# Keys by token: tensor-engine transposes in place of vector-engine block transposes

## The chip, the cores and the metric

The kernel runs on one core of a Trainium2 chip. The metric is the device time of one execution in microseconds, lower is better. The core has a tensor engine (TensorE, "PE" in the profile, with its weight loads as "PEld"), a vector engine (VectorE, "DVE"), a scalar engine (ScalarE, "ACT"), GpSimd ("POOL") and SyncE ("SP"), which issues the transfers. Each engine takes its instructions in order from its own queue and waits for the others by semaphores.

## What is computed

One layer of a hybrid decoder trunk on 2048 tokens of width 1024 in float32: RMS norm, one input projection to 3072 columns, two mixers side by side, an output projection with a residual add, a gated per-layer embedding and a final norm. The mixer that the change touches is a gated linear recurrence with four heads of 128 channels, cut to its core:

```python
b = jnp.cumsum(logf, axis=3)                 # log decays within a chunk
qe, ke = q * jnp.exp(b), k * jnp.exp(-b)
scores = where(causal, einsum('bhnck,bhnsk->bhncs', qe, ke), 0.0)
o_intra = einsum('bhncs,bhnsv->bhncv', scores, v)
dS = einsum('bhnsk,bhnsv->bhnkv', k * jnp.exp(b_last - b), v)
S[n + 1] = decay[n] * S[n] + dS[n]           # state of a head, 128 x 128
o = o_intra + einsum('bhnck,nbhkv->bhncv', qe, S)
```

The keys are needed in two layouts: with channels on the partitions for the scores, and with tokens on the partitions for the state update `dS`, because a matrix product sums over the partitions of both operands.

## The kernel before

The input projection and both mixers run first, for 1024 tokens at a time (`half(0)` and `half(1)`); a second phase does the output projection, the embedding and the last norm for 16 tiles of 128 tokens. Projections take float32 values in two parts of 12 significant bits, so that each product is three TensorE passes (`mm3`, lines 85 to 87).

In each half a list of units is worked through: `v` (values), `g` (output gates), `a` (the other mixer, four channel blocks), `fq` (decays, keys and queries of one head). A unit `fq` loads its weights and calls `unit_b(w, j, b)` for the two blocks of 512 tokens (`b` is 0 and 1), so there are 2 x 4 x 2 = 16 calls. One call does this:

- the projection `f` on TensorE; two sigmoids on ScalarE (`f` and `kn`, lines 431 and 432);
- a long run of VectorE work: the decay `f` (line 433), running products `cp` (438), their reciprocal `rc` (440), and at the end the scaled keys `kn` (455), 128 channels x 512 tokens;
- `transpose_blocks` (lines 199 to 204, used with `u2T` in the second phase too): 16 VectorE instructions, each of which transposes four 32x32 blocks, make `kT` from `kn` (lines 456 and 457);
- the projection `q` and its scaling;
- `scores` (line 469): four products of `kn` and `q` into the PSUM tile `sc`, masked into `sc_buf` by VectorE;
- `states` (line 477): four products of `kT` and the values into `ds` (line 480), then a chain over four chunks between ScalarE (`sp`, line 488) and VectorE (`state`, 489);
- `outputs` (line 493): products of `sc_buf` with the values and of `q` with the states (lines 496 and 499), and a norm;
- `finish` (line 513): four TensorE transposes `oT` (line 519), read by VectorE (`yb`, 521), and a transfer to DRAM.

The short pieces run some groups of products later: `after(n, fn)` notes a function, `tick()` at the end of each group runs what is due. That is the order in which the program is written. The order in which each engine's queue is filled is laid by a planner when the kernel is built: it simulates the engines with its own costs and takes, among what is ready by them, the piece that was written first. A product whose input is not ready by the planner's reckoning is so put behind others that are; on the chip the order is fixed.

PSUM has eight banks: three for projections (`pj`), three for `sc`, `ds`, `o` and the gates of unit `a` (`gl`), two in `tp`, which hold `oT` and the broadcast scales `rs` of the norm. A tile of a pool waits until the reader of the tile that had the buffer before it is done.

Of the kernel before, what the change touches and what calls it, by code (L numbers as in the profile page):

```python
# [8 lines left out]
F32 = mybir.dt.float32  # L9
# [7 lines left out]
# column blocks of the input projection, in the order in which the host lays them out  # L17
UNITS = [("v", 0), ("v", 1), ("fq", 0), ("g", 0), ("a", 0), ("fq", 1), ("a", 1), ("fq", 2), ("a", 2), ("g", 1), ("a", 3),
         ("fq", 3)]
P = 128  # L20
T = 2048
D = 1024
KT = D // P
NB = 512
# [3 lines left out]
# power of two that keeps the (masked) scores of later keys with earlier queries in range  # L28
DOWN = 2.0 ** -64
# columns of the packed per-channel vectors  # L30
# [5 lines left out]
def hymba_block(ctx: ExitStack, tc: tile.TileContext, x, xT, pT, w_in, vecs, rg_w, w_out, w_gate,  # L36
# [35 lines left out]
    def split(hi, lo, src, lo_eng):  # L72
        """src = hi + lo exactly, each with 12 significant bits."""
        nc.scalar.activation(hi, src, AF.Identity)  # L74
        lo_eng.tensor_tensor(lo, src, hi.bitcast(F32), ALU.subtract)  # L75

    def load_split(hi, lo, src, lo_eng, pool, tag, bufs, name):
        """hi + lo = src of DRAM, by way of a buffer of the given pool and tag."""
        raw = pool.tile(list(hi.shape), F32, tag=tag, name=f"raw_{name}", bufs=bufs)
        nc.sync.dma_start(raw, src)  # L80
        split(hi, lo, raw, lo_eng)

    def mm3(acc, lh, ll, rh, rl, first, last):
        """acc += (lh + ll)^T (rh + rl), without the product of the two low parts (under 2^-24)."""
        nc.tensor.matmul(acc, lhsT=lh, rhs=rh, start=first, stop=False)  # L85
        nc.tensor.matmul(acc, lhsT=lh, rhs=rl, start=False, stop=False)  # L86
        nc.tensor.matmul(acc, lhsT=ll, rhs=rh, start=False, stop=last)  # L87

# [13 lines left out]
    # the tensor engine reaches its full clock only after a while of work: products of constants until data is there  # L102
# [22 lines left out]
    def small_vectors():  # L125
        nc.sync.dma_start(vec, vecs[:, 0:NV])
        # softplus(-lambda) = max(-lambda, 0) + 2 atanh(y / (2 + y)), y = exp(-|lambda|)
        lam = vec[:, V_LAM:V_LAM + NH]
        c = [c1.tile([P, NH], F32, name=f"c{i}") for i in range(5)]
        nc.vector.tensor_scalar(c[0], lam, -1.0, 0.0, ALU.mult, ALU.max)  # L130
        nc.vector.tensor_scalar(c[1], lam, 0.0, None, ALU.min)
        nc.vector.tensor_tensor(c[1], c[1], c[0], ALU.subtract)
        nc.vector.scalar_tensor_tensor(c[1], lam, 0.0, c[0], ALU.max, ALU.add)
        nc.scalar.activation(c[2], c[1], AF.Exp, scale=-1.0)
        nc.vector.tensor_scalar(c[3], c[2], 2.0, None, ALU.add)
        nc.vector.reciprocal(c[3], c[3])
        nc.vector.tensor_tensor(c[2], c[2], c[3], ALU.mult)
        nc.vector.tensor_tensor(c[3], c[2], c[2], ALU.mult)
        nc.vector.tensor_scalar(c[4], c[3], 1.0 / 17, 1.0 / 15, ALU.mult, ALU.add)
        for n in (13, 11, 9, 7, 5, 3, 1):  # L140
            nc.vector.tensor_tensor(c[4], c[4], c[3], ALU.mult)
            nc.vector.tensor_scalar(c[4], c[4], 1.0 / n, None, ALU.add)
        nc.vector.tensor_tensor(c[4], c[4], c[2], ALU.mult)
        nc.vector.scalar_tensor_tensor(c[4], c[4], 2.0, c[0], ALU.mult, ALU.add)
        nc.vector.tensor_scalar(sp8, c[4], 8.0, None, ALU.mult)
        nc.vector.tensor_scalar(nsp8, c[4], -8.0, None, ALU.mult)
        # first row of softmax(hg_lb)
        l0, l1 = vec[:, V_LB0:V_LB0 + NH], vec[:, V_LB1:V_LB1 + NH]
        nc.vector.tensor_tensor(c[0], l0, l1, ALU.max)
        nc.vector.tensor_tensor(c[1], l0, c[0], ALU.subtract)  # L150
        nc.vector.tensor_tensor(c[2], l1, c[0], ALU.subtract)
        nc.scalar.activation(c[1], c[1], AF.Exp)
        nc.scalar.activation(c[2], c[2], AF.Exp)
        nc.vector.tensor_tensor(c[2], c[1], c[2], ALU.add)
        nc.vector.reciprocal(c[2], c[2])
        nc.vector.tensor_tensor(lb, c[1], c[2], ALU.mult)
        nc.vector.tensor_scalar(omlb, lb, -1.0, 1.0, ALU.mult, ALU.add)

    # Gate weights of the 8 blocks of 64 channels, in two parts: both gates side by side in the columns, and the
    # same rows twice, for the two parts of the block's channels.  # L160
# [9 lines left out]
    def inv_rms(pool, ss, tag):  # L170
        """1 / sqrt(mean + eps) of each partition, from the columns of ss that add up to its sum of squares."""
        ms = pool.tile([P, 1], F32, tag="ms", name=f"ms_{tag}", bufs=2)
        if ss.shape[1] > 1:
            nc.vector.tensor_reduce(ms, ss, AX.X, ALU.add)
            ss = ms
        nc.vector.tensor_scalar(ms, ss, 1.0 / D, EPS, ALU.mult, ALU.add)  # L176
        rs = pool.tile([P, 1], F32, tag="rs", name=f"rs_{tag}", bufs=2)
        nc.gpsimd.tensor_tensor(rs, ms, neg_half[:, 0:1], ALU.pow)  # L178
        return rs

    def rms_scale(pool, src, tag, junk):
        """1 / sqrt(mean(src^2) + eps) of each partition's row."""
        ss = pool.tile([P, 1], F32, tag="ss", name=f"ss_{tag}", bufs=2)
        nc.scalar.activation(junk, src, AF.Square, accum_out=ss)
        return inv_rms(pool, ss, tag)

    def resident(src, n, pool, kt, name, raw_pool, raw_tags):
        """Column half n of src in two parts, as [128, 512] tiles by row block. They may arrive in places of later
        tiles."""
        his, los = [], []  # L190
        for k in range(kt):
            his.append(pool.tile([P, NB], F32R, tag=f"hi{k}_{n}", name=f"{name}_hi{k}_{n}"))
            los.append(pool.tile([P, NB], F32R, tag=f"lo{k}_{n}", name=f"{name}_lo{k}_{n}"))
            rp, tag, bufs = raw_tags[k] if isinstance(raw_tags[k], tuple) else (raw_pool, raw_tags[k], 1)
            load_split(his[k], los[k], src[k * P:(k + 1) * P, n * NB:(n + 1) * NB],
                       nc.vector if k % 2 else nc.gpsimd, rp, tag, bufs, f"{name}{k}_{n}")
        return his, los

    def transpose_blocks(dst, src):
        """dst[:, k] = src[:, k]^T, 128 x 128, by 32 x 32 blocks on the vector engine."""  # L200
# [11 lines left out]
    # Short pieces of tensor engine work whose inputs take a while run some groups of products later.  # L212
# [3 lines left out]
    def after(n, fn):  # L216
        later.append((clock[0] + n, fn))
# [27 lines left out]
    def prep_u(hf, tt, rs=None):  # L245
        """u = rms_norm(x) of 128 tokens, channel-major, in two parts."""
# [20 lines left out]
    def load_w(hf, n, between=None, raw_pool=None, *raw_tags):  # L267
        """A block of 256 columns of the input projection, in two parts."""
# [12 lines left out]
    def begin():  # L281
        """The first values need no scaled input: of two tiles, x times the norm's weight, in two parts, and the
        scales, by which the products are multiplied."""
# [26 lines left out]
    def half(hf):  # L310
# [15 lines left out]
        def v_tiles(w, pair, t2):  # L326
            """Values of two heads for 256 tokens, token-major."""
# [31 lines left out]
        def unit_a(w, j):  # L359
# [20 lines left out]
            def recur():  # L380
                # a = exp(-8 r sp); 1 - a^2 = tanh(8 r sp) (1 + a^2)
# [19 lines left out]
            for b in range(2):  # L401
# [9 lines left out]
                # the two parts of each 64 channels, one above the other  # L411
# [11 lines left out]
        def unit_b(w, j, b):  # L423
            """Gated linear recurrence of head j on one block of 512 tokens, in chunks of 128 whose decays are
            taken relative to the middle of the chunk."""
# [8 lines left out]
            # running products of the decays from the start of each 64  # L434
# [19 lines left out]
            # keys  # L454
            nc.vector.scalar_tensor_tensor(kn, kn, omlb[:, j:j + 1], rc, ALU.mult, ALU.mult)
            kT = bp.tile([P, NB], F32, tag="kT", name=f"kT_{nm}", bufs=2)
            transpose_blocks(kT.rearrange("p (n s) -> p n s", n=4), kn.rearrange("p (n s) -> p n s", n=4))
            tick()
            # queries
# [9 lines left out]
            def scores():  # L469
# [5 lines left out]
                after(1, lambda: states(sc))  # L475

            def states(sc):
# [15 lines left out]
            def outputs(sc, sps):  # L493
# [6 lines left out]
                # norm over the head's values, per token  # L500
# [59 lines left out]
    def load_y(tt, pool, bufs, raw_pool, raw_tag):  # L560
        """One tile of mixer outputs in two parts, and of the residual stream."""
# [57 lines left out]
    def gate(tt, uh, ul, h):  # L619
# [10 lines left out]
        # the last tile ends on narrower pieces, whose chain is shorter  # L630
# [24 lines left out]
    def split_u2(tt, last):  # L655
        """u2T of a tile in two parts; those of the last tiles take the place of mixer outputs."""
# [33 lines left out]
def _layout(inp):  # L690
# [5 lines left out]
    # by 64 channels: the two gates' weights side by side, in the other order for every second block  # L696
# [37 lines left out]
```

## Time and profile before

| | us |
|---|---|
| median of 3 runs | 1103.26 |
| lowest and highest of them | 1098.7 to 1104.31 |
| profiled execution: span from first to last instruction | 1104.0 |
| its TensorE busy | 1044.5 |
| its VectorE busy | 814.9 |
| its ScalarE busy | 451.1 |
| its GpSimd busy | 278.3 |

The profiled execution is an execution of its own; its time is told by its span, which holds the whole of it. Busy time is the time in which an engine has an instruction under way. Matrix products overlap in the pipeline, so a busy TensorE is not TensorE at its peak. An idle engine costs time only where the work that sets the end waits for it.

### The profile page before, as it was taken

The page shows a single profiled execution, that of the slowest core. Times are in us where ns is not written, and L with a number is a line of the kernel's source. Part 1 is how long each engine was busy: PE and PEld are TensorE (multiplying, and loading weights), DVE is VectorE, ACT ScalarE, POOL GpSimd, SP SyncE. Part 2 cuts the span into 40 slices and gives each one's busy share as a digit, 9 for nine tenths or more (in the row PEclk, how much of TensorE's full clock was granted, in tenths as well). Part 3 has the DMA queues.
Part 4 walks back from the last instruction along what each step waited for, and adds up shares of the span by engine and source line. Part 5 has one row for each costly group of instructions (what it writes and reads, how often), then busy time and mean ns, then how long its engine had stood idle before and what let it go on. Part 6 is the DMA issues. An engine that isn't in the chain of part 4 may idle for free.

```text
span 1104.0 us, 13904 instructions
## 1 busy us (share of the span) xinstructions
PE 1044.5 (95%) x5128; PEld 874.3 (79%) x5128; DVE 814.9 (74%) x1629; ACT 451.1 (41%) x763; POOL 278.3 (25%) x238
## 2 busy tenths in 40 slices
PE   8899899898898999999989899899999999999997
PEld 7888788687777998788778788667888888888886
DVE  5846946979799706965979969899766666666664
ACT  4546336455556325535545226642222222222222
POOL 4131221222222132221222216651112221111110
PEclk8999999999899999999999999899999999999999
DMA  8421111111135211111112128441122222211101
GB/s 324 135 77 39 58 58 39 57 58 58 57 115 204 102 58 58 58 58 39 58 48 67 33 82 273 128 158 63 64 84 77 72 67 67 67 63 57 43 29 49
DMA packets 55267, 91.10 MB, mean 83 GB/s; under 512 B 4640, under 2 KB 25120, under 8 KB 55200
## 3 DMA queue, kind: packets, MB, share of 16 engines
q1 hardware_dynamic: 55200, 90.22, 24.0%
q8 instruction: 40, 0.66, 0.2%
q14 instruction: 27, 0.22, 0.1%
HBM read 73.43 MB, written 16.78 MB: 82 GB/s over the span
## 4 chain that ended last, share of the span: by engine, by line
PE 54%; DVE 30%; DMA 4%; ACT 4%; issue 4%; POOL 2%; SPq 0%; POOLq 0%; DVEq 0%; ACTq 0%
DVE kT L203 7%; PE g L86 6%; PE g L87 6%; PE g L85 6%; PE o L87 4%; PE o L86 4%; PE o L85 4%; DVE rc L440 4%; PE v L87 2%; PE v L86 2%; DMA raw_w<-in_w_in 2%; PE v L85 2%; PE ga L87 2%; PE ga L85 2%; PE ga L86 2%
## 5 line engine op out<-in xcount | busy, mean ns | idle before, releaser
L75 POOL TENSOR_TENSOR wlo<-raw_w,whi 128x512 fp32r<-128x512 f32 x92 | 133.5, 1461 | 330.8 <-ACT whi L74 330.8
L203 DVE STREAM_TRANSPOSE u2T<-u 32x256 f32<-32x256 f32 x256 | 111.7, 436 | 3.8
L87 PE MATMUL o<-wo_hi,yl 128*128 128x512 f32 x256 | 102.4, 401 | 3.5 <-POOL yl L75 3.5
L85 PE MATMUL o<-wo_hi,yh 128*128 128x512 f32 x256 | 101.3, 396 | 0.7 <-ACT yh L74 0.7
L86 PE MATMUL o<-wo_lo,yh 128*128 128x512 f32 x256 | 101.6, 397 | 0.0
L86 PE MATMUL g<-wg_lo,u2uh 128*128 128x512 f32 x224 | 89.2, 398 | 2.6 <-DVE wg_lo L75 2.6
L85 PE MATMUL g<-wg_hi,u2uh 128*128 128x512 f32 x224 | 89.2, 398 | 1.4 <-ACT wg_hi L74 1.4
L87 PE MATMUL g<-wg_hi,u2ul 128*128 128x512 f32 x224 | 88.6, 396 | 0.0
L74 ACT ACTIVATE whi<-raw_w 128x512 fp32r<-128x512 f32 x96 | 57.7, 624 | 72.4 <-DMA raw_w<-in_w_in 63.6
L203 DVE STREAM_TRANSPOSE kT<-kn 32x128 f32<-32x128 f32 x256 | 77.4, 302 | 3.4
L488 ACT ACTIVATE sp<-state,dec 128x128 f32<-128x128 f32 x60 | 23.9, 400 | 115.5 <-DVE state L489 66.0
L87 PE MATMUL v<-whi,ul 128*128 128x256 f32 x224 | 63.8, 286 | 3.4 <-DVE ul L75 3.4
L75 POOL TENSOR_TENSOR yl<-raw_y,yh 128x512 fp32r<-128x512 f32 x32 | 45.4, 1422 | 84.1 <-ACT yh L74 84.1
L86 PE MATMUL v<-wlo,uh 128*128 128x256 f32 x224 | 63.5, 284 | 0.6 <-POOL wlo L75 0.6
L85 PE MATMUL v<-whi,uh 128*128 128x256 f32 x224 | 63.6, 285 | 0.0
L87 PEld LDWEIGHTS o<-wo_hi,yl 128*128 128x128 f32 x256 | 48.6, 190 | 15.1 <-POOL yl L75 4.0
L406 DVE TENSOR_SCALAR xc<-xa,vec 128x512 f32<-128x512 f32 x16 | 11.4, 711 | 64.7 <-ACT xa L404 64.5
L85 PEld LDWEIGHTS o<-wo_hi,yh 128*128 128x128 f32 x256 | 48.6, 190 | 12.6 <-ACT yh L74 1.2
L86 PEld LDWEIGHTS o<-wo_lo,yh 128*128 128x128 f32 x256 | 48.5, 189 | 12.2
L178 POOL TENSOR_TENSOR rs_f<-ms_f,neg_half 128x1 f32<-128x1 f32 x16 | 8.8, 551 | 190.2 <-DVE ms_f L176 177.2
L74 ACT ACTIVATE yh<-raw_y 128x512 fp32r<-128x512 f32 x32 | 19.9, 629 | 86.3 <-issue 53.9
L641 ACT ACTIVATE gt<-gt 128x512 f32<-128x512 f32 (+1 forms) x33 | 20.2, 611 | 83.0 <-DVE gt L640 83.0
(219 smaller groups left out, 2956.9 us busy)
## 6 DMA issues: line engine op xcount, KB each, us to landing
raw_w<-in_w_in SPq DMA_DIRECT2D x96, 256.0 KB, 2.9
xcm<-in_xT SPq DMA_DIRECT2D x18, 512.0 KB, 4.0
xt<-in_x SPq DMA_DIRECT2D x16, 512.0 KB, 5.4
raw_y<-y_dram SPq DMA_DIRECT2D x32, 256.0 KB, 2.8
h<-in_x SPq DMA_DIRECT2D x16, 512.0 KB, 3.4
out<-h SPq DMA_DIRECT2D x15, 512.0 KB, 2.6
y_dram<-ga SPq DMA_DIRECT2D x16, 256.0 KB, 2.4
y_dram<-yb SPq DMA_DIRECT2D x16, 256.0 KB, 2.1
```

Of the source, the lines that this page charges most:

```text
L74: nc.scalar.activation(hi, src, AF.Identity)
L75: lo_eng.tensor_tensor(lo, src, hi.bitcast(F32), ALU.subtract)
L85: nc.tensor.matmul(acc, lhsT=lh, rhs=rh, start=first, stop=False)
L86: nc.tensor.matmul(acc, lhsT=lh, rhs=rl, start=False, stop=False)
L87: nc.tensor.matmul(acc, lhsT=ll, rhs=rh, start=False, stop=last)
L178: nc.gpsimd.tensor_tensor(rs, ms, neg_half[:, 0:1], ALU.pow)
L203: nc.vector.transpose(dst[32 * j:32 * j + 32, :, 32 * i:32 * i + 32], src[32 * i:32 * i + 32, :, 32 * j:32 * j + 32])
L406: nc.vector.tensor_scalar(xc[:, s], xa[:, b * NB:b * NB + NB], cw[:, 0:1], vec[:, V_CONVB + j:V_CONVB + j + 1], ALU.mult, ALU.add)
L440: nc.vector.reciprocal(rc, cp)
L488: nc.scalar.activation(sp, state[j], AF.Identity, scale=dec[:, n])
L641: nc.scalar.activation(gt, gt, AF.Sigmoid)
```

## The change

`transpose_blocks` is no longer called in `unit_b`. In `scores`, behind the mask, four TensorE transposes of 128x128 take `kn` to a PSUM tile `pk` of the pool `tp`, and one ScalarE copy takes `pk` to `kT` in SBUF. `states` gets `kT` as an argument. `transpose_blocks` stays for `u2T`. Comments are taken out elsewhere.

```diff
             nc.vector.scalar_tensor_tensor(kn, kn, omlb[:, j:j + 1], rc, ALU.mult, ALU.mult)
-            kT = bp.tile([P, NB], F32, tag="kT", name=f"kT_{nm}", bufs=2)
-            transpose_blocks(kT.rearrange("p (n s) -> p n s", n=4), kn.rearrange("p (n s) -> p n s", n=4))
             tick()
...
                 nc.vector.copy_predicated(sc, keep.bitcast(U32), psc.rearrange("p (n t) -> p n t", n=4))
-                after(1, lambda: states(sc))
-
-            def states(sc):
+
+                pk = tp(f"kT_{nm}")
+                for c in cs:
+                    nc.tensor.transpose(pk[:, c], kn[:, c], ident)
+                kT = bp.tile([P, NB], F32, tag="kT", name=f"kT_{nm}", bufs=2)
+                nc.scalar.activation(kT, pk, AF.Identity)
+                after(1, lambda: states(sc, kT))
+
+            def states(sc, kT):
                 pds = gl(f"ds_{nm}")
                 for n, c in enumerate(cs):
                     nc.tensor.matmul(pds[:, c], lhsT=kT[:, c], rhs=vt[:, 4 * b + n, hc], start=True, stop=True)
```

## Rows read from the trace of the kernel before

**Rows 1.** The page's busy time of each engine: us, share, instructions.

```profile
PE 1044.5 (95%) x5128; PEld 874.3 (79%) x5128; DVE 814.9 (74%) x1629; ACT 451.1 (41%) x763; POOL 278.3 (25%) x238
```

**Rows 2.** The page's chain that ended last, by engine and by line.

```profile
PE 54%; DVE 30%; DMA 4%; ACT 4%; issue 4%; POOL 2%; SPq 0%; POOLq 0%; DVEq 0%; ACTq 0%
DVE kT L203 7%; PE g L86 6%; PE g L87 6%; PE g L85 6%; PE o L87 4%; PE o L86 4%; PE o L85 4%; DVE rc L440 4%; PE v L87 2%; PE v L86 2%; DMA raw_w<-in_w_in 2%; PE v L85 2%; PE ga L87 2%; PE ga L85 2%; PE ga L86 2%
```

**Rows 3.** Windows: stretch, length, busy PE PEld DVE ACT POOL, clock, DMA, GB/s.

```profile
60.00:360.00 300.00, 279.22 (x1381) 234.39 (x1380) 233.60 (x476) 152.43 (x234) 78.19 (x62) 0.98 0.22 76
360.00:660.00 300.00, 285.65 (x1531) 245.57 (x1530) 218.25 (x453) 126.10 (x198) 69.57 (x51) 0.98 0.17 57
```

**Rows 4.** Waits of TensorE: us in total, times, longest.

```profile
PE ds L480 <- DVE kT L203: 22.3, 13, 3.6
PE sc L472 <- DVE kn L455: 10.2, 6, 2.0
```

**Rows 5.** Timeline of TensorE: start, us, instruction, idle before and its releaser.

```profile
196.96 1.13 PE L480 MATMUL ds<-v,kT 128*128 128x128 f32 x8 [0.57 <-DVE kT L203]
...
214.19 1.13 PE L472 MATMUL sc<-q,kn 128*128 128x128 f32 x8 [1.56 <-DVE kn L455]
...
220.31 1.16 PE L480 MATMUL ds<-v,kT 128*128 128x128 f32 x8 [2.97 <-DVE kT L203]
...
614.64 2.08 PE L480 MATMUL ds<-v,kT 128*128 128x128 f32 x8 [3.07 <-DVE kT L203]
```

**Rows 6.** Timeline of VectorE between 190 and 222 us.

```profile
191.77 5.04 DVE L203 STREAM_TRANSPOSE kT<-kn 32x128 f32<-32x128 f32 x16
196.84 0.67 DVE L433 TENSOR_SCALAR f<-f,omlb,lb 128x512 f32<-128x512 f32 x1
...
197.57 2.17 DVE L394 TENSOR_TENSOR i<-i,th 128x1024 f32<-128x1024 f32 x1
...
213.30 0.74 DVE L455 SCALAR_TENSOR_TENSOR kn<-kn,omlb,rc 128x512 f32<-128x512 f32 x1
...
215.22 5.04 DVE L203 STREAM_TRANSPOSE kT<-kn 32x128 f32<-32x128 f32 x16
```

**Rows 7.** Windows of the six half-clock stretches, first and sum, columns as above.

```profile
136.52:139.94 3.42, 3.42 (x14) 2.94 (x13) 1.99 (x6) 0.40 (x1) 1.02 (x1) 0.50 0.00 0
...
sum 23.91, PE 22.91 PEld 20.11 DVE 21.70 ACT 2.53 POOL 2.71; mean PE 3.82 PEld 3.35 DVE 3.62 ACT 0.42 POOL 0.45
```

**Rows 8.** Groups of instructions: busy us, mean ns, idle before and releasers.

```profile
L203 DVE STREAM_TRANSPOSE kT<-kn 32x128 f32<-32x128 f32 x256 | 77.4, 302 | 3.4
...
L519 PE MATMUL oT<-ident,on 128*128 128x128 f32 x60 | 9.1, 272 | 0.0
...
L404 ACT ACTIVATE xa<-xa 128x512 f32<-128x512 f32 x14 | 8.3, 591 | 9.5 <-PE xa L87 9.3
```

**Rows 9.** Timeline of ScalarE, around 194 and around 212 us.

```profile
194.30 1.06 ACT L391 ACTIVATE th<-th 128x1024 f32<-128x1024 f32 x1
...
209.69 0.40 ACT L488 ACTIVATE sp<-state,dec 128x128 f32<-128x128 f32 x1 [2.06 <-DVE state L489]
...
213.41 0.40 ACT L488 ACTIVATE sp<-state,dec 128x128 f32<-128x128 f32 x1 [1.30 <-DVE state L489]
214.73 1.28 ACT L415 ACTIVATE xp<-xc 64x512 fp32r<-64x512 f32 x2 [0.92 <-DVE xc L409]
```

**Rows 10.** Timeline of TensorE: two groups of `oT`, the next `sc`.

```profile
228.88 0.60 PE L519 MATMUL oT<-ident,on 128*128 128x128 f32 x4
229.32 0.39 PE L499 MATMUL o<-sp,q 128*128 128x128 f32 x2
...
238.73 0.60 PE L519 MATMUL oT<-ident,on 128*128 128x128 f32 x4
...
251.68 1.05 PE L472 MATMUL sc<-q,kn 128*128 128x128 f32 x8
```

**Rows 11.** Timeline of VectorE: the reader of the second.

```profile
244.69 0.75 DVE L521 SCALAR_TENSOR_TENSOR yb<-oT,vec,gb 128x512 f32<-128x512 f32 x1
```

## The prediction

> **What bounds the kernel now.** I read the page first. TensorE is busy 95% of the span and VectorE 74% [rows 1], so over the whole run TensorE is nearly full; but the chain that ended last spends 30% of its time on VectorE, and its largest single entry is `kT`, the sixteen block transposes of line 203 [rows 2]. Both can be true only if TensorE is the limit for most of the time and VectorE for short stretches, so the next view is busy time by stretch. From 60 to 660 us, where all 16 calls of `unit_b` lie, TensorE is idle 20.8 + 14.4 = 35.2 us [rows 3]. The view of waits names who ends that idleness: line 480 (`ds`, which reads `kT`) waits 22.3 us in 13 places, line 472 (`sc`, which reads `kn`) 10.2 us in 6 [rows 4]. 32.5 of the 35.2 us are thus VectorE's keys coming late. All else that holds TensorE there is 2.7 us.
>
> The timeline of TensorE shows the form of it [rows 5]. It comes in pairs, once for each head: on the first block of 512 tokens `ds` waits little (0.57 at 196.96). On the second block `sc` waits 1.56 at 214.19, short output products and two projection products follow, and then `ds` waits 2.97 at 220.31. The last of these second waits is 3.07 at 614.64. I read all 13: the seven of second blocks add up to 18.8, the six of first blocks to 3.5. The near constant 3 us has a plain reading in VectorE's own timeline [rows 6]: `kn` starts at 213.30 and is followed by one convolution step and one gate product, then come sixteen transposes from 215.22 that take 5.04 us, and `ds` starts in the very moment they end (220.3). TensorE ran out of work at 220.31 - 2.97 = 217.34, some 2 us after `sc` ended (214.19 + 1.13 = 215.32), so 3 us are left over. The order was laid down as if the transposes were cheaper than they are.
>
> The gaps cost a second time. Directly after six of these pairs, or between their two waits, the granted clock is 0.50 for a stretch [rows 7]: the stretches add up to 23.9 us with TensorE busy 22.9 us in them, at the level of 1.2 GHz in place of 2.4. At full clock that work takes half, so 22.9 / 2 = 11.5 us are lost. Idle and half clock together: 22.3 + 10.2 + 11.5 = 44.0 us is what late keys cost in this execution.
>
> **The change part by part.** I sum against the profiled execution, whose span is 1104.0; the median of the runs shown, 1103.26, lies 0.1% below, so I forecast on the same scale.
>
> *Removed: 256 block transposes.* 77.4 us of VectorE at 302 ns each, 16 x 0.302 = 4.8 in sum and 5.04 by the clock for a call [rows 6, 8]. They aren't worth 77 us, because TensorE works under most of them. They are worth the waits that end on them: the 22.3 us of `ds` go as far as they are a wait for line 203. Term: -22.3.
>
> *Moved earlier: what stood behind the transposes on VectorE.* Between 190 and 222 VectorE has hardly a free moment (the transposes at 191.77 are followed at 196.84 by the next block's `f`, and so on to `kn` at 213.30 [rows 6]). Without the 5 us at 191.77, the chain to the second block's `kn` can start up to 5 us earlier, but `i` (line 394) in that queue needs the square root that ScalarE ends at 194.30 + 1.06 = 195.36 [rows 9], against its start at 197.57 now, so in an unchanged order only about 2.2 us are won. The `sc` wait there is 1.56, so it could vanish. On the other side the planner lays the order again: it takes its own, too small, cost of the transposes out and may bring `sc` forward with `kn`, which keeps the wait. Bounds 0 and -10.2; nothing tells which is nearer, so I take the middle. Term: -5.
>
> *Added on TensorE: 64 transposes of 128x128 f32.* The kernel has the same instruction already, `oT` at line 519, four to a call: the mean is 272 ns [rows 8], but they overlap: four start at 228.88 and the next product starts at 229.32, 0.44 us later [rows 10]. 16 x 0.45 = 7.2. TensorE is the limit, so all of it counts. Term: +7.2. The upper bound is no overlap at all, 64 x 0.272 = 17.4.
>
> The Trainium skill speaks against this part: "TensorE: Matmul & The Clock Gate", section "PE-mode transpose", puts such a transpose at about 275 ns inside a kernel. The row's 272 ns agrees, but the starts in the trace lie 0.11 apart. By the page's figure as an estimate the term would be 64 x 0.275 = 17.6 in place of 7.2, and the result about 1091.
>
> *Added on ScalarE: 16 copies of 128x512 from PSUM.* Line 404 is that copy, 591 ns [rows 8]: 9.5 us in all, on an engine busy 152 and 126 of 300 us [rows 3]. Being busy little hides the work, not the delay: `ds` now waits for transposes, then copy, and ScalarE's queue is in order. Ahead of the copy in a first block stands that square root, which ends at 195.36; `ds` there is at 196.96 now [rows 5], so a copy behind it (195.4 to 196.0) is ready in time, and one behind another 0.6 us piece a few tenths late. In a second block there are the last `sp` of the block before (213.41) and the two `xp` at 214.73, which waited 0.92 for VectorE [rows 9]. With `sc` at about 213, transposes until 214.5 and a copy of 0.6, `kT` is there between 215.2 and 216.6, while TensorE has those 2 us of output products to run. Bounds for a call: 0 (hidden by those products) and 1.3 (the copy stands behind an `sp` that waited 1.30). The first is nearer, since both queues give room; I take 0.25 on the mean. Term: 16 x 0.25 = +4.
>
> *The two buffers of `tp`.* The new transposes share them with `oT`, whose reader is `yb` on VectorE. The `oT` at 238.73 is the last of its head and is read from 244.69 to 245.4; the next head's first `sc` stands at 251.68 [rows 10, 11]. So the buffers are free 6 us before they are wanted, and I take nothing; if that cover went, a late `yb` would stop TensorE itself for up to the 6 us between 238.73 and 244.69.
>
> *The clock.* With the 3 us hole gone and the `sc` hole halved, I expect about four of the six half-speed stretches to go. Bounds 0 and -11.5. Term: -7.
>
> Sum: 1104.0 - 22.3 - 5 + 7.2 + 4 - 7 = 1080.9, so **1081**. The boundary between the halves and everything from 660 us on have their own work; I let them move up unchanged.
>
> **The rivals.**
> *All of it comes back.* `sc` never waits, the copy is always hidden, the clock never falls: 1104.0 - 22.3 - 10.2 - 11.5 + 7.2 = 1067. For it: VectorE loses 77 of its 234 + 218 = 452 us between 60 and 660 us [rows 3]. Against: the holes exist because the order is planned on costs that differ from the chip's, and reciprocals and scans stay.
> *The hole stays half open.* `sc` waits as before and `ds` waits 1 us for the copy in each call: -22.3 + 16 + 7.2, with half the clock losses back (-5.7): 1099. For it: ScalarE waits 1.3 and 2.1 us in front of `sp` in just these stretches [rows 9].
> *Slower: the wait only changes hands.* The copy is planned behind an `sp` or `xp` that hangs on VectorE, so `ds` waits in total as long as now (22.3 us, 1.4 for each call), and TensorE has the transposes on top: 1104.0 + 7.2 = 1111. It decides from a mean wait of 1.3 us for each call: then -22.3 + 16 x 1.3 + 7.2 = +5.7, over half a per cent. Against: only the copies of second blocks meet such a queue.
> *Transposes do not overlap here.* If the four run one after the other as their 272 ns say, the term is 17.4, not 7.2: 1081 + 10.2 = 1091. Against it stands the pitch in [rows 10]. The Trainium skill's section named above gives the same result.
> That VectorE is not relieved at all can be left out: line 203 keeps only `u2T`.
>
> **How the numbers follow.** Half a per cent (5.5 us) is about what a measurement of this kernel tells from no change. Chances: the forecast (1072 to 1090) 0.58; all of it (1063 to 1072) 0.12; half open (1090 to 1104) 0.16, of which half lies below 1097.7; wait changes hands (1105 to 1115) 0.08; transposes in series 0.06. Faster by over 0.5%: 0.58 + 0.12 + 0.08 + 0.06 = 0.84. Slower by over 0.5%: three quarters of the changed hands, 0.06. Within: 0.10. The range 1066 to 1099 leaves out some of the best case, the upper part of the half-open one and the slower one, near 2 in 10; the likeliest alone is 1072 to 1090.
>
> **What would show it.** In the profile of the changed kernel: no `kT` at line 203, VectorE busy near 815 - 77 = 737; 64 single transposes into a `kT` tile on TensorE with starts 0.11 apart; 16 ScalarE copies near 0.6 us. Right, if line 480 waits under 6 us in all, names ScalarE as releaser, and the granted clock from 60 to 660 is 0.99 or more. The `sc` term is right if line 472 waits between 3 and 8 us. Wrong, if `ds` waits over 1 us for the copy in most calls, if a transpose waits for `yb`, or if a new wait appears in stretches that were full before, because the order was laid anew.

## The result and the profile after

The changed kernel takes 1090.0 us (median of 4 runs, 1087.67 to 1091.96) against 1102.41 us (4 runs, 1098.7 to 1104.31) for the kernel before on the same chip: a ratio of 0.9876, 95% interval 0.9852 to 0.9899. That is 13.7 us faster (0.0124 x 1104), inside the predicted range, where 23 us were forecast. The profiled execution has a span of 1088.5 us, 15.5 less than before.

The page's busy time and its chain, beside [rows 1, 2]:

```profile
PE 1043.3 (96%) x5192; PEld 878.2 (81%) x5192; DVE 739.3 (68%) x1373; ACT 459.4 (42%) x779; POOL 272.1 (25%) x238
...
PE 73%; DVE 15%; DMA 5%; ACT 3%; issue 2%; POOL 1%; SPq 1%; POOLq 0%; DVEq 0%; ACTq 0%
```

VectorE has lost 75.6 us and its share of the chain is halved. TensorE's part of the chain went from 54% to 73%. The windows of the two stretches, beside [rows 3], and the view of TensorE's waits from 60 to 660 us, beside [rows 4]:

```profile
60.00:360.00 300.00, 287.59 (x1481) 244.57 (x1480) 206.79 (x380) 161.12 (x248) 78.96 (x64) 0.99 0.25 83
360.00:660.00 300.00, 291.86 (x1564) 251.37 (x1563) 182.55 (x306) 133.99 (x216) 68.01 (x52) 0.99 0.19 61
```

```profile
PE sc L470 <- DVE kn L455: 16.7, 7, 3.1
PE o L503 <- ACT sp L492: 2.1, 3, 1.4
```

TensorE's idle time there fell from 35.2 to 12.4 + 8.1 = 20.5 us. The wait of `ds` for the transposed keys, 22.3 us before, is gone altogether. But the other wait on late keys, `sc` for `kn`, rose from 10.2 to 16.7 us, and it is nearly all that is left: seven waits, one at the second block of each of seven heads. TensorE's timeline around the pair of [rows 5] shows it:

```profile
190.49 1.05 PE L470 MATMUL sc<-q,kn 128*128 128x128 f32 x8
191.38 0.60 PE L476 MATMUL kT<-ident,kn 128*128 128x128 f32 x4
...
196.85 1.06 PE L484 MATMUL ds<-v,kT 128*128 128x128 f32 x8
...
206.87 1.13 PE L470 MATMUL sc<-q,kn 128*128 128x128 f32 x8 [2.39 <-DVE kn L455]
207.84 0.60 PE L476 MATMUL kT<-ident,kn 128*128 128x128 f32 x4
208.28 0.61 PE L500 MATMUL o<-v,sc_buf 128*128 128x128 f32 x4
...
212.62 1.06 PE L484 MATMUL ds<-v,kT 128*128 128x128 f32 x8
```

The four transposes stand directly behind `sc`, the next product starts 208.28 - 207.84 = 0.44 us after them, and neither `ds` shows a wait. The keys do come sooner, as VectorE's timeline shows, beside [rows 6]:

```profile
187.14 0.74 DVE L455 SCALAR_TENSOR_TENSOR kn<-kn,omlb,rc 128x512 f32<-128x512 f32 x1
...
191.57 1.22 DVE L438 TENSOR_TENSOR_SCAN cp<-f,d 128x512 f32<-128x512 f32 x1
193.53 0.06 DVE L393 MEMSET th<- 128x1 f32 x1 [0.73 <-ACT th L391]
193.62 1.22 DVE L394 TENSOR_TENSOR i<-i,th 128x1024 f32<-128x1024 f32 x1
...
205.99 0.74 DVE L455 SCALAR_TENSOR_TENSOR kn<-kn,omlb,rc 128x512 f32<-128x512 f32 x1
```

For comparison, the first block's `sc` in TensorE's timeline of the kernel before:

```profile
192.34 1.05 PE L472 MATMUL sc<-q,kn 128*128 128x128 f32 x8
```

Count from that `sc` in each kernel. The second block's `kn` started 213.30 - 192.34 = 21.0 us behind it before, and 205.99 - 190.49 = 15.5 us now: 5.5 us sooner, near the 5.04 us of one call's block transposes. TensorE, though, reaches the second block's `sc` (its start less its wait) 212.63 - 192.34 = 20.3 us behind it before, and 204.48 - 190.49 = 14.0 us now: 6.3 us sooner. The newly laid order has fewer projection products between the two: from the first block's `ds` to the second block's `sc` there were 64, and now there are 29. So TensorE asks earlier by more than the keys are earlier, and the wait grows from 1.56 to 2.39 us. The other six heads that wait show the same in the timelines: on the mean of the seven, the keys come 4.8 us sooner and TensorE asks 5.7 us sooner, and seven times the difference of 0.93 is the 6.5 us by which the wait grew.

The stretches of half clock between 60 and 660 us, the first of three and their sum, beside [rows 7]:

```profile
127.33:130.74 3.41, 3.41 (x19) 3.41 (x18) 1.02 (x3) 1.40 (x3) 0.00 (x0) 0.50 0.26 98
...
sum 10.23, PE 10.23 PEld 10.23 DVE 4.64 ACT 4.09 POOL 0.00; mean PE 3.41 PEld 3.41 DVE 1.55 ACT 1.36 POOL 0.00
```

Six stretches have become three, and the loss went from 11.5 to 10.2 / 2 = 5.1 us. The tile `kT` in the changed kernel (durations are minimum, median and maximum in ns, then first and last start in us):

```profile
L476 PE MATMUL kT<-ident,kn x64: 270/273/421, 111.1 to 617.7; 128*128 128x128 f32 x64
L478 ACT ACTIVATE kT<-kT x16: 577/584/607, 113.1 to 620.6; 128x512 f32<-128x512 f32 x16
```

The second phase only moved up. The product of line 85 that waits for `yh` stands in TensorE's timeline of the kernel before at

```profile
704.44 0.50 PE L85 MATMUL o<-wo_hi,yh 128*128 128x512 f32 x1 [0.73 <-ACT yh L74]
```

and in that of the changed kernel at

```profile
688.63 0.50 PE L85 MATMUL o<-wo_hi,yh 128*128 128x512 f32 x1 [0.45 <-ACT yh L74]
```

15.8 us earlier, which is the whole difference of the spans. The terms by the profile are -22.3 (`ds`), +6.5 (`sc`), +7.2 (transposes, taken at the prediction's 16 x 0.45) and -6.3 (clock), in sum -14.9. The small other waits rose from 2.7 to 20.5 - 16.7 = 3.8 us, which makes it -13.8: 2 us of the 15.8 aren't accounted for.

### The profile page after: what moved, and what is told of

It reads as the page before. It is cut to its first block, busy times and chain, and to the rows that moved or that the text cites. A ratio compares the mean times of both kernels' runs of the same rounds, so it can differ in the third digit from the quotient of the medians.

```text
span 1088.5 us, 13796 instructions
## 1 busy us (share of the span) xinstructions
PE 1043.3 (96%) x5192; PEld 878.2 (81%) x5192; DVE 739.3 (68%) x1373; ACT 459.4 (42%) x779; POOL 272.1 (25%) x238
## 4 chain that ended last, share of the span: by engine, by line
PE 73%; DVE 15%; DMA 5%; ACT 3%; issue 2%; POOL 1%; SPq 1%; POOLq 0%; DVEq 0%; ACTq 0%
PE g L86 7%; PE g L87 7%; PE g L85 6%; PE o L87 4%; PE o L86 4%; PE o L85 4%; DVE rc L440 3%; PE v L87 2%; PE v L86 2%; PE v L85 2%; PE q L86 2%; PE q L85 2%; PE q L87 2%; PE f L87 2%; PE f L86 2%
## 5 line engine op out<-in xcount | busy, mean ns | idle before, releaser
L75 POOL TENSOR_TENSOR wlo<-raw_w,whi 128x512 fp32r<-128x512 f32 x92 | 125.6, 1379 | 303.6 <-ACT whi L74 303.2
L440 DVE RECIPROCAL rc<-cp 128x512 f32<-128x512 f32 x16 | 53.6, 3348 | 0.2
L86 PEld LDWEIGHTS g<-wg_lo,u2uh 128*128 128x128 f32 x224 | 42.3, 189 | 13.2 <-DVE wg_lo L75 2.6
```

The source lines that it names most:

```text
L440: nc.vector.reciprocal(rc, cp)
```

## The experiments

Ratios are to the kernel before on the same chip, with 95% intervals; the changed kernel has 0.9876 [0.9852, 0.9899]. A difference of ratios is turned into time with 1104 us. Waits are those of TensorE from 60 to 660 us. Two questions come out of the profile: whether the wait of `sc` can be had back by asking later, or only goes to whoever asks VectorE next; and whether the gain comes from VectorE's relief, or from `ds` no longer hanging on VectorE. The expectations call the rival answers theories. A tick is one call of `tick()`, at the end of a group of products; `after(n, fn)` runs `fn` n ticks later.

### Is the wait of `sc` a matter of the order?

**Scores of the second block two ticks later**, on the changed kernel.

```diff
-            after(2 if b == 0 else 1, scores)
+            after(2 if b == 0 else 3, scores)
```

> The changed kernel, but the scores of the second block are noted two groups of products later (after(3)), so that the planned order on TensorE puts the next gate projection and the output products of the first block ahead of them, about 2.2 us of work (two products of 0.226 us and sixteen short ones of 0.11). Theory A (the order reaches the scores 2 to 3 us before VectorE has the keys, and nothing else is short): the 16.7 us of waits at sc fall under 5, the three half-clock stretches behind them mostly go (about 1.7 us each), and the time is 1070 to 1078. Theory B (VectorE's throughput is the limit in these stretches): the wait comes back at ds, at the outputs or at the next head's scores, and the time is 1086 to 1094.

Measured: 1090.02 us, 0.9867 [0.9838, 0.9896], no different from the changed kernel, as theory B has it. Its waits:

```profile
PE o L500 <- DVE sc_buf L472: 10.5, 7, 2.4
PE o L503 <- ACT sp L492: 7.6, 7, 1.6
```

The wait of `sc` has gone, and 10.5 + 7.6 = 18.1 us stand at the output products of the first block, which the order now puts in front. They hang on the same late VectorE (`sc_buf` is its mask, and `sp` follows its `state`). Asking VectorE for something else first moves the wait and saves nothing.

**Scores and outputs both later**, on the changed kernel, with ticks of half a group inside the projections. The first four lines are put behind each k's products in `project`:

```diff
+                if k == KT // 2 - 1:
+                    clock[0] += 0.5
+                    run_due()
+                    clock[0] -= 0.5
...
-                after(1, lambda: outputs(sc, sps))
+                after(3 if b == 0 and j < 3 - hf else 1, lambda: outputs(sc, sps))
...
-            after(2 if b == 0 else 1, scores)
+            after(2 if b == 0 else 3.5 if j < 3 - hf else 1, scores)
```

> The changed kernel, planned so that pure projection work stands where TensorE waits for the keys: the scores of the second block come 14 products (3.2 us) later and the first block's outputs some 24 products later, behind them; the last head of each half stays as it was. Theory A (VectorE is only behind the order by 2 to 3 us at one place in each head, and has slack afterwards): waits at sc and o together fall under 6 us, the half-clock stretches behind them go, and the time is 1068 to 1080. Theory B (VectorE's throughput limits these stretches whatever the order): the waits come back at ds, at the outputs or at the next head's scores, and the time is 1086 to 1095.

Measured: 1069.46 us, 0.9682 [0.9650, 0.9714]: 21 us under the changed kernel, as theory A has it. Its windows, its waits, and its pair of `sc` in TensorE's timeline:

```profile
60.00:360.00 300.00, 295.08 (x1576) 252.93 (x1576) 211.09 (x392) 163.39 (x249) 78.48 (x64) 1.00 0.26 85
360.00:640.00 280.00, 279.06 (x1465) 238.70 (x1464) 175.01 (x292) 133.03 (x215) 70.13 (x53) 1.00 0.20 66
```

```profile
PE o L507 <- ACT sp L496: 2.2, 2, 1.7
PE sc L474 <- DVE kn L459: 1.0, 2, 0.7
PE ds L488 <- ACT kT L482: 1.0, 1, 1.0
```

```profile
184.68 1.05 PE L474 MATMUL sc<-q,kn 128*128 128x128 f32 x8
...
201.69 1.05 PE L474 MATMUL sc<-q,kn 128*128 128x128 f32 x8
...
666.41 0.50 PE L85 MATMUL o<-wo_hi,yh 128*128 128x512 f32 x1 [0.47 <-ACT yh L74]
```

The second `sc` comes 17.0 us after the first, against 14.0 in the changed kernel, and waits for nothing. The gap is filled with projection products, not with other customers of VectorE. All TensorE waits from 60 to 660 us together are 5.7 us in place of 20.4, and no stretch of half clock is left there (5.1 us): 14.7 + 5.1 = 19.8 of the 22.2 us by which line 85's product moved up.

**Both a tick further, without half ticks.**

```diff
-                after(1, lambda: outputs(sc, sps))
+                after(4 if b == 0 and j < 3 - hf else 1, lambda: outputs(sc, sps))
...
-            after(2 if b == 0 else 1, scores)
+            after(2 if b == 0 else 4 if j < 3 - hf else 1, scores)
```

> As the run before, but the second block's scores and the first block's outputs are both noted four groups later, so the scores come 26 products (5.9 us) later than in the changed kernel and the outputs some 50 products. Theory A: no more is won than by 3.2 us, 1068 to 1080, as the keys were only 2 to 3 us late. Theory C (what is put off must be done in the same head, and the work piles up at its end): waits appear at the next head's outputs or transposes, 1080 to 1092. Theory B: 1086 to 1095.

Measured: 1067.32 us, 0.9669 [0.9638, 0.9701], the lowest of all kernels here and below the range of each theory, though not clear of the run before, whose interval overlaps. It is called the best kernel below. TensorE is idle 300 - 297.6 = 2.4 us in the first window:

```profile
60.00:360.00 300.00, 297.61 (x1594) 256.71 (x1594) 208.04 (x392) 161.05 (x247) 79.34 (x64) 0.99 0.26 85
```

**The same on the kernel before, without the change.**

```diff
-                after(1, lambda: outputs(sc, sps))
+                after(5 if b == 0 and j < 3 - hf else 1, lambda: outputs(sc, sps))
...
-            after(2 if b == 0 else 1, scores)
+            after(2 if b == 0 else 5 if j < 3 - hf else 1, scores)
```

> The kernel before, all transposes on VectorE, with the scores of the second block noted so late that they stand behind the second gate projection of the next unit, 23 products (5.2 us) later, and ds and the first block's outputs some 24 products behind them; the last head of each half stays as it was. Theory A (the order alone was at fault, VectorE has time enough on the whole): the 32.5 us of waits for keys fall under 10 us and the time is 1068 to 1080, as good as the late order with the change. Theory B (VectorE's 77 us of transposes fill it, so the work put off shows as waits later in the head): 15 us or more of waits on VectorE stay, 1083 to 1098.

Measured: 1096.58 us, 0.9911 [0.9885, 0.9937], as theory B has it. So the order alone is worth some 10 us, and the later order by itself doesn't make the fast kernel. In such an order (a tick longer here than in the best kernel) the change brings (0.9911 - 0.9669) x 1104 = 27 us, twice its 13.7 in the plain one. Of the 36.5 us between the kernel before and the best one, 9.8 come with the order alone, 13.7 with the change alone, and the other 13 only with both. The waits of the kernel before in this order are spread over many customers of VectorE, the first two being:

```profile
PE rg L373 <- DVE xp L416: 6.8, 3, 3.3
PE sc L472 <- DVE kn L455: 4.2, 2, 2.3
```

**Only `states` of the second block later, on the kernel before.** It asks whether 3 us of slack for `ds` would have done the change's work.

```diff
-                after(1, lambda: states(sc))
+                after(4 if b == 1 and j < 3 - hf else 1, lambda: states(sc))
```

> The kernel before, with its transposes on VectorE, but the states of the second block are noted three groups of products later, so that some 28 products (6 us) stand between its scores and ds; the last head of each half stays as it was. Theory A (the 3 us hole at ds was a matter of order): 6 of the 7 second waits go, about 16 us, and half of the clock losses, 6 us: 1080 to 1088 without any tensor-engine transpose. Theory B (VectorE is behind, and the wait goes to whoever asks it next): over half of the wait shows up at sc, o or the next ds, 1094 to 1104.

Measured: 1094.35 us, 0.9929 [0.9903, 0.9954], at the lower end of theory B. The profiled execution took 1101.34 us, 7 us over the median of ten (1092.7 to 1101.6), so its waits are those of a longer one. In it `ds` waits 5.8 us for `kT` in place of 22.3, but others take over:

```profile
PE sc L472 <- DVE kn L455: 13.0, 7, 3.0
PE rg L373 <- DVE xp L416: 6.7, 3, 3.0
PE ds L480 <- DVE kT L203: 5.8, 7, 3.1
```

As long as VectorE is late, whoever asks it next waits. Still, this one line brings 7.8 us (0.0071 x 1104), over half of the 13.7 of the change in the plain order, with all transposes still on VectorE: part of the hole at `ds` was a matter of order.

### Is it VectorE's relief that counts, and how much of it?

**VectorE keeps its transposes beside the new ones**, into a tile that nothing reads.

```diff
             nc.vector.scalar_tensor_tensor(kn, kn, omlb[:, j:j + 1], rc, ALU.mult, ALU.mult)
+            spare = bp.tile([P, NB], F32, tag="rc", name=f"spare_{nm}", bufs=1)
+            transpose_blocks(spare.rearrange("p (n s) -> p n s", n=4), kn.rearrange("p (n s) -> p n s", n=4))
```

> The changed kernel, in which VectorE does its sixteen block transposes of each call as well, into a buffer that nobody reads: 77 us of VectorE work are back, but ds reads the keys that TensorE and ScalarE made. Theory A (the gain is that ds no longer ends on transposes that take 5 us by the clock; the time that VectorE wins is taken up by the new order): ds waits stay at 0, sc waits are 8 to 17 us, the time 1088 to 1097. Rival (the gain is VectorE's relief): keys come 5 us later, waits at sc go to 25 us or more, the time is 1103 to 1112.

Measured: 1117.44 us, 1.0120 [1.0096, 1.0144]: 27 us over the changed kernel and 13 over the kernel before. I had expected that most of the gain came from `ds` no longer hanging on the transposes; that fell. `ds` hardly waits here, and nearly all of it is back at `sc`:

```profile
PE sc L472 <- DVE kn L455: 29.3, 7, 5.4
...
PE ds L486 <- ACT kT L480: 1.8, 1, 1.8
```

The windows of its seven half-clock stretches, the sum:

```profile
sum 37.40, PE 30.71 PEld 30.82 DVE 34.64 ACT 10.19 POOL 0.56; mean PE 4.39 PEld 4.40 DVE 4.95 ACT 1.46 POOL 0.08
```

12.6 us more of `sc` waits and 30.7 / 2 - 5.1 = 10.3 us more of half clock are 22.9 of the 27 us. The gain of the change thus hangs on VectorE's relief; how much of the 77 us it takes, the next two runs show. That `ds` reads another engine's tile is worth little by itself.

**The change for second blocks only**: first blocks keep the block transposes.

```diff
-            transpose_blocks(kT.rearrange("p (n s) -> p n s", n=4), kn.rearrange("p (n s) -> p n s", n=4))
+            if b == 0:
+                transpose_blocks(kT.rearrange("p (n s) -> p n s", n=4), kn.rearrange("p (n s) -> p n s", n=4))
...
+                if b == 1:
+                    pk = tp(f"kT_{nm}")
+                    for c in cs:
+                        nc.tensor.transpose(pk[:, c], kn[:, c], ident)
+                    nc.scalar.activation(kT, pk, AF.Identity)
```

> Half of the change: only the second block's keys go over TensorE and ScalarE, the first block's stay block transposes on VectorE. Theory A (the gain is the ds wait of the second block; waits at sc stay as before, as the first block's transposes are in the plan): 18.8 us of waits go, 3.6 us of TensorE come, a third of the clock loss goes (4 us): 1082 to 1089, no worse than the whole change. Theory B (VectorE's total work before the second block's keys sets the sc wait): the first block's 5 us of transposes show at sc, 20 us or more there, 1094 to 1100.

Measured: 1084.84 us, 0.9822 [0.9792, 0.9852]. In the plain order half of the change does at least as well as the whole (the intervals touch), as theory A has it. Its waits are those of `sc` (11.7), and `ds` of first blocks (4.7):

```profile
PE sc L473 <- DVE kn L455: 11.7, 7, 2.0
PE ds L486 <- DVE kT L203: 4.7, 6, 2.1
```

TensorE's waits add up to 21.7 us, near the 20.4 of the changed kernel; what this kernel has ahead of it are 32 transposes less (3.6 us by the prediction's price) and one stretch of half clock in place of three.

This run also tests where the growth of the `sc` wait came from. With the first block's transposes left in place, 57 to 64 projection products stand again between the first block's `ds` and the second block's `sc` in these seven heads (57 to 64 in the kernel before, 29 to 31 in the changed one), and the wait stays near its old 10.2 us. So it is the removal of the first block's transposes that brings both the keys and the demand for them forward.

**The same half with the later order** (the two lines of the best kernel above).

> Half of the change (the second block's keys over TensorE, the first block's on VectorE) with the late order of the scores and outputs, as in the run with four groups. Theory A (with the late order VectorE is not short, and only TensorE's work counts): 3.6 us less than the whole change in that order, 1061 to 1066. Theory B (VectorE has 39 us more to do and the sc wait for the second block stays, since its scores stand where they stood in the kernel before): 8 us or more of waits at sc, 1070 to 1080.

Measured: 1083.15 us, 0.9793 [0.9747, 0.9839], clearly behind the whole change in that order (0.9669) and 3 us above the range of theory B, whose 8 us of waits at `sc` are there (8.1). The first blocks' 39 us of VectorE, less the transposes that TensorE does for them, are worth about 14 us (0.0124 x 1104) once TensorE does not ask early for what comes behind them, and nothing that shows when it does.

### What do the added operations cost?

**Transposes twice**, the second time over the first.

```diff
-                for c in cs:
+                for c in cs + cs:
                     nc.tensor.transpose(pk[:, c], kn[:, c], ident)
```

> The changed kernel with each of the 64 TensorE transposes done twice into the same place. Theory A (TensorE is the limit and four transposes cost their starts, 0.44 us): 16 x 0.44 = 7 us more, 1095 to 1099. Rival 1 (each costs its whole 272 ns): 17 us more, 1105 to 1110. Rival 2 (they vanish under waits for the keys): 1088 to 1092.

Measured: 1098.65 us, 0.9937 [0.9913, 0.9962]: 64 more transposes cost 0.0061 x 1104 = 6.7 us, 0.42 for four, give or take 4 us by the two intervals. The 0.45 of the prediction fits, and the 17.4 us of 64 x 0.272 do not.

**Transposes twice in the best order**, where TensorE has hardly a gap.

> The late order with four groups, and each TensorE transpose done twice. TensorE is now nearly never idle in these stretches, so nothing can hide the work. Theory A (0.44 us for four): 7 us more than the late order alone, 1072 to 1077. Rival (part of it vanishes): under 1070. Rival (272 ns each): over 1082.

Measured: 1074.92 us, 0.9725 [0.9678, 0.9771]: 0.0056 x 1104 = 6.2 us over the best kernel, 0.39 for four, give or take 6 us. Within the noise they cost the same with TensorE full.

**No transposes and no copy**: `states` multiplies a constant in place of the keys, so this kernel leaves the keys out of the state update.

```diff
-                pk = tp(f"kT_{nm}")
-                for c in cs:
-                    nc.tensor.transpose(pk[:, c], kn[:, c], ident)
-                kT = bp.tile([P, NB], F32, tag="kT", name=f"kT_{nm}", bufs=2)
-                nc.scalar.activation(kT, pk, AF.Identity)
+                kT = keep.rearrange("p n t -> p (n t)")
```

> The changed kernel without any transposition: states takes a constant triangle in place of the keys by token, so neither TensorE transposes nor the copy are there, and ds doesn't depend on the keys. Theory A (the added price is the 7 us of TensorE): 1080 to 1085, with the sc waits still at 10 to 20 us. Rival (the path through PSUM and ScalarE costs more than its TensorE time, by buffers of tp and ScalarE's queue): under 1077. Second rival (the transposes were under waits): 1088 to 1092.

Measured: 1087.77 us, 0.9854 [0.9830, 0.9879], only 2.4 us under the changed kernel, with overlapping intervals, above the range of theory A. The 7 us were not all given back: TensorE's waits from 60 to 660 us add up to 24.3 us here against 20.4 in the changed kernel, with `sc` at 18.5 against 16.7. In the plain order TensorE's relief, too, partly turns into waiting for `kn`.

**The copy on VectorE** in place of ScalarE.

```diff
-                nc.scalar.activation(kT, pk, AF.Identity)
+                nc.vector.tensor_copy(kT, pk)
```

> The changed kernel with the copy of the transposed keys on VectorE instead of ScalarE, 16 x about 0.7 us = 11 us of VectorE work. Theory A (VectorE is behind at the second block's keys, and everything added in front of them there costs, as 77 us cost 27): waits at sc and ds together 17 to 25 us, 1091 to 1100. Rival (the copies fall into VectorE's slack): 1087 to 1091.

Measured: 1089.77 us, 0.9851 [0.9804, 0.9898], the same as the changed kernel and the time of the rival, not of theory A. Its waits:

```profile
PE sc L470 <- DVE kn L455: 8.4, 6, 1.7
PE ds L484 <- DVE kT L478: 8.2, 7, 2.0
```

8.4 + 8.2 = 16.6 us, the changed kernel's 16.7 split in two. In the plain order the choice of engine for the copy decides where TensorE waits and not how long. In the later order it wasn't tried.

## Why the prediction was right, and where it was not

**What bounds the kernel: right.** Late keys were the limit, and VectorE the reason. With its 77 us put back the kernel is 27 us slower. But in the plain order the second blocks' half of the 77 us gives the whole gain.

**`ds` waits, -22.3: right.** None is left, and the hole of 3 us in each second block is closed.

**`sc` waits, -5: wrong, and the step that made the forecast 9 us too low.** The prediction saw that "the planner lays the order again" and "may bring `sc` forward with `kn`, which keeps the wait", and set the bounds at 0 and -10.2. It measured +6.5. What was missing was a bound on the other side. The earlier keys and the demand for them are set by two clocks: VectorE's real time and the planner's costs. In the pair shown VectorE gained 5.5 us, the planner moved `sc` up by 6.3, and a wait that was there could grow. The prediction's 2.2 us for `i` (line 394) held as such: counted from the first block's `sc`, it started 197.57 - 192.34 = 5.2 us behind before and 193.62 - 190.49 = 3.1 now. But the new order puts `cp` (line 438) ahead of `i`, and `i` itself is 0.95 us shorter, so that `kn` gained more than `i`. By the prediction's own signs ("a new wait appears ... because the order was laid anew") this is the case that it named and didn't price. The later order shows what the term could be: there 1 us of `sc` wait or none remains, and the time falls to 1067 to 1069, the forecast of the rival in which all of it comes back.

**Transposes, +7.2: right.** The row that decided was the distance of starts, 0.44 us for four, and two kernels with doubled transposes measured 0.42 and 0.39. The Trainium skill ("TensorE: Matmul & The Clock Gate", section "PE-mode transpose") gives about 275 ns for one of bf16; single ones of f32 take 273 ns here, but by that figure as an estimate 64 more would have cost 17.6 us, and they cost 6.2 to 6.7. That the measured 1090 lies next to the 1091 of the rival in which transposes don't overlap is a coincidence: the 9 us came from `sc`.

**The copy, +4: too much.** No `ds` waits for it: 0. The queue that the prediction feared is there, in ScalarE's timeline of the changed kernel:

```profile
209.92 1.29 ACT L415 ACTIVATE xp<-xc 64x512 fp32r<-64x512 f32 x2 [0.26 <-DVE xc L409]
211.23 0.60 ACT L478 ACTIVATE kT<-kT 128x512 f32<-128x512 f32 x1
```

The copy starts 3.4 us after the first transpose (207.84), behind an `xp` that had waited 0.26 us for VectorE. But the order put output products and projection work in front of `ds`, which starts at 212.62 without a wait. So the wait didn't change hands to ScalarE; it went back to VectorE's `kn`. Output products wait 2.1 us for `sp` on ScalarE, which they did not before; with the copy on VectorE that is 1.9 us, so it isn't the copy that holds them.

**`tp` buffers, 0: right.** No transpose into `kT` waits for `yb`.

**Clock, -7: right** (-6.3), though by three stretches of six and not four. The three follow `sc` waits that stayed: where these are gone, in the kernel with half ticks, there is no stretch of half speed from 60 to 660 us. It is not the whole of it: the best kernel, without any `sc` wait, has one at 336.73, behind waits of 0.38 and 1.35 us for the `v` products of the second half.

Two errors partly cancelled: `sc` was 11.5 us worse than taken, the copy 4 better. Of the rivals, the half-open one (1099) comes nearest in kind, since a hole is left at each second block, but it stands at `sc` and not at `ds`.

Why VectorE runs 2 to 3 us behind the planned order at the second block's `kn` is open. That the planner takes VectorE's instructions there to be cheaper than they are was argued, not shown: the timelines show the order that it laid, and no run shows its costs.

## What to carry to other kernels

When work is taken off an engine that is late, look for the next instruction that waits for the same engine, and price it on both sides: an order that is laid anew can bring the demand forward by more than the supply. The relief is realised when all consumers of the late engine are put behind work that doesn't need it; moving one of them puts another in front. The order does not replace the relief: without the change a like order gave 10 us here, on top of the change 23 (0.0207 x 1104). Price short back-to-back products by the distance of their starts, not by their durations.

## What was not expected of the hardware

A VectorE product of two 128x1024 tiles changed its duration with its neighbours. In the groups of VectorE from 60 to 660 us, before and then after:

```profile
L394 DVE TENSOR_TENSOR i<-i,th 128x1024 f32<-128x1024 f32 x7 | 15.6, 2225 | 0.2
```

```profile
L394 DVE TENSOR_TENSOR i<-i,th 128x1024 f32<-128x1024 f32 x7 | 8.6, 1225 | 2.3 <-ACT th L391 2.1
L386 DVE TENSOR_TENSOR i<-i,xc 128x1024 f32<-128x1024 f32 x7 | 8.5, 1215 | 0.0
```

Before, it took 2225 ns on the mean; after, 1225, like the other product of that size. The instruction is the same. Before, the one at 197.57 to 199.74 ran while GpSimd made `wlo`; after, it is over at 194.84, 0.3 us after GpSimd's `wlo` begins. GpSimd's timeline of the kernel before and of the kernel after:

```profile
195.96 2.70 POOL L75 TENSOR_TENSOR wlo<-raw_w,whi 128x512 fp32r<-128x512 f32 x2 [16.91 <-ACT whi L74]
200.86 2.92 POOL L75 TENSOR_TENSOR wlo<-raw_w,whi 128x512 fp32r<-128x512 f32 x1 [2.20 <-ACT whi L74]
```

```profile
194.55 2.70 POOL L75 TENSOR_TENSOR wlo<-raw_w,whi 128x512 fp32r<-128x512 f32 x2 [17.38 <-ACT whi L74]
```

Before, GpSimd's piece ends at 195.96 + 2.70 = 198.66, and the VectorE product 1.08 us later, a little less than its undisturbed duration. All seven before start under a `wlo` and end 1.07 to 1.09 us after it; none of the seven after starts under one. That fits a VectorE instruction that stands still until GpSimd is done, 15.6 - 8.6 = 7.0 us in sum here. The Trainium skill ("SBUF — State Buffer", section "SBUF: two separate sides") states it so: of a VectorE instruction with two SBUF inputs and a GpSimd one that reads SBUF, the later blocks fully until the first is done. The trace agrees in these rows; in the kernel with both kinds of transposes, where VectorE is back at its old pace, the product takes 2223 ns again. The kernel before in the later order has both cases in one execution: the four products that start under a `wlo` take 2.16 to 2.31 us, the three others 1.21 to 1.23. The other way round, the single `wlo` at 200.86 starts under VectorE's scan of line 395 (200.35 to 202.69) and takes 2.92 us, where two in a row took 2.70. All this is read from overlaps and was not tried by itself.
